# A hybrid attention block with SwiGLU: the down product on scaled f16 halves instead of fp32r

## The chip, the cores and the metric

One core of one Trainium2 chip runs the whole kernel in one launch. The metric is device time in microseconds (us) of that core. Five engines work side by side: TensorE (PE, with PEld for its weight loads), VectorE (DVE), ScalarE (ACT), GpSimd (POOL) and SyncE (SP), which here issues the transfers.

## What is computed

The reference is one encoder block over 2048 tokens (and 16 meta tokens) of width 1024, all in float32. The change concerns the last part, the feed-forward network (FFN) of inner width 2816:

```
h = rms_norm(x, attn_norm_g[l])
proj = jnp.einsum('bld,de->ble', h, w_in[l])
...
mixed = jnp.concatenate([out_a, out_b], axis=-1)
x = x + jnp.einsum('ble,ed->bld', mixed, w_out[l])
h = rms_norm(x, ffn_norm_g[l])
g = jnp.einsum('bld,df->blf', h, w_gate[l])
u = jnp.einsum('bld,df->blf', h, w_up[l])
x = x + jnp.einsum('blf,fd->bld', jax.nn.silu(g) * u, w_down[l])
```

out_a is grouped-query attention of 8 heads, out_b differential attention of 4 heads; both normalise queries and keys and turn them by rotary tables.

## The kernel before

The kernel runs through four stages. Every product of float32 numbers is made of three matmuls on halves: an operand x is cast to a short type (the high half) and the cast's error x − high is cast again (the low half); high·high, high·low and low·high are summed. `split` (L114 to L116) does this: the cast on ACT (L112), the subtract on POOL or DVE (L116). Products on f16 halves need the operands scaled into f16's range, products on fp32r halves don't.

- Input projection (0 to 480 us): 16 token tiles of 128 rows (and one of 16), and for each six units of 384 columns of w_in; `proj` makes 24 matmuls a unit, `post` norms and rotates, and SP stores queries, keys and values to DRAM (L281, L330 to L335).
- Attention (480 to 1670 us), whose order of instructions a planner in the program sets. The change doesn't touch it.
- Output projection (1670 to 1884 us): 16 token tiles, 48 fp32r matmuls each (L1285). Meanwhile the weights w_gate and w_up are read once to find a scale: 32 loads of 704 KB (`squares`, L1238) with an ACT square each that sums along a row (L1239); `weights_scale` (L1243 to L1253) adds up the sums with a matmul against ones and takes a power of two near 1/sqrt of the total (POOL's pow at L1248, then a mask). `wsc` holds it.
- FFN (1884 to 3304 us): two halves b of the tokens (1024 each), and in each 22 tiles f of 128 inner columns, so 44 steps. A step loads w_gate, w_up and w_down of its tile (`wload`, L1323 to L1331: SP loads 512 KB into a raw tile, ACT scales gate and up by `wsc`, ACT casts, POOL subtracts), makes 96 matmuls of 128x512 for gate and up in f16 (L1379), forms silu(g)·u with a tanh on ACT (L1381) and two DVE products (L1382, L1383), splits it into fp32r halves, and multiplies the previous step's tile by its w_down: 48 fp32r matmuls (`down`, L1340), three for each of 16 outputs of 128x512, each of which DVE adds to the running sum y (L1342).

A scheduler orders the instructions of each engine from the program as written, outside the attention, so matmuls of `down` are mixed among those of gate and up. Tiles are given out from rings: four tiles for f16 weights of gate and up, four raw tiles, two for w_down's halves and two for the activation's:

```
rings = dict(w=[er[0], we[0], er[1], wk_[0]], d=[we[1], wk_[1]], a=[we[2], wk_[2]], y=[we[3], wk_[3]],
             r=[slots[id(z)] for t in (NT - 2, NT - 1) for z in mxt[t]])
```

A tile can be written again when its last reader is done: a raw tile after POOL's subtract, a w_down tile after the last matmul of its `down`. Sums of `down` go to a ring of three PSUM tiles (`psD`). The names that the profile shows are those of the memory that a tile lies in: e, kt, qa, qb are also the attention's buffers; qa and qb hold raw weights, e and kt the halves; psd is a sum of `down`, pg one of gate or up, th the activation, pj a projected unit, xt a tile of x, cs the rope table.

## Time and profile before

| what | us |
|---|---|
| median of 3 runs (lowest, highest) | 3316.16 (3311.18, 3320.15) |
| the profiled execution, its own time | 3310.24 |
| span of the profile | 3308.4 |
| PE busy | 3145.7 (95% of the span) |
| PEld, DVE busy | 2069.5, 2056.2 |
| ACT, POOL busy | 1639.2, 1639.3 |

The span is the time from the first to the last instruction of the profiled execution; its own time is 2 us longer. Busy shares are means over stages that differ: the page's slices show PE full from the output projection on, and a granted clock of 0.9 or more of full speed in every slice. The rows below are read stage by stage.

### The profile page before, as it was taken

The numbers are of one execution on the slowest core, as the hardware profiler recorded it, in microseconds if no ns is written. First come the engines' busy times: TensorE is split into PE (matmuls) and PEld (weight loads), VectorE is DVE, ScalarE is ACT, GpSimd is POOL, SyncE is SP. The second block draws the span as 40 slices with busy tenths as digits, with TensorE's granted clock in tenths as the row PEclk, the third lists the DMA queues.
The fourth block names the chain that finished last, engine by engine and source line by source line (L and its number), as shares of the span: only waits on it lengthen the run. The fifth ranks groups of instructions, "written<-read, shape, count | busy, mean of one in ns | idle before, by whom it ended". The sixth has DMA issues, their size and how long they took to land.

```text
span 3308.4 us, 57942 instructions
## 1 busy us (share of the span) xinstructions
PE 3145.7 (95%) x23043; PEld 2069.5 (63%) x23043; DVE 2056.2 (62%) x3656; ACT 1639.2 (50%) x1991; POOL 1639.3 (50%) x1597
## 2 busy tenths in 40 slices
PE   8999988989988898888889999999999999999999
PEld 7999975655555565555568755555555555555555
DVE  7555568888888889888865334444444544444445
ACT  6333328888887888888866222222222322222220
POOL 6888866767676677676721133232232323232231
PEclk9999999999999999999999999999999999999999
DMA  5322233343243334433467511111111511111111
GB/s 168 72 68 68 67 85 74 78 109 88 73 111 81 84 86 100 88 83 74 107 236 259 165 58 55 42 58 42 54 52 45 174 50 51 45 58 39 57 45 51
DMA packets 503359, 281.35 MB, mean 85 GB/s; under 512 B 330704, under 2 KB 478624, under 8 KB 502576
## 3 DMA queue, kind: packets, MB, share of 16 engines
q1 hardware_dynamic: 501376, 275.14, 30.6%
q8 instruction: 181, 2.97, 0.4%
q10 hardware_dynamic: 1712, 2.51, 0.3%
q14 instruction: 90, 0.74, 0.1%
HBM read 168.44 MB, written 39.93 MB: 63 GB/s over the span
## 4 chain that ended last, share of the span: by engine, by line
PE 72%; DVE 11%; ACT 6%; issue 5%; DMA 4%; POOL 1%; SPq 0%; DVEq 0%; ACTq 0%; POOLq 0%
PE pg L1379 27%; PE psd L1340 14%; PE pl L269 10%; PE sy L482 4%; PE ob L594 4%; PE oa L570 3%; DVE e L489 3%; ACT et L555 2%; DVE mna L502 2%; PE ps L1285 2%; PE sy L498 2%; PE sy L512 2%; PE sy L513 2%; DVE e L536 2%; DMA wq<-in_w_up_dram 1%
## 5 line engine op out<-in xcount | busy, mean ns | idle before, releaser
L1342 DVE TENSOR_TENSOR y<-psd,y 128x512 f32<-128x512 f32 x704 | 484.8, 691 | 551.0 <-PE psd L1340 549.8
L561 POOL TENSOR_TENSOR hl<-et,hl 128x1024 f16<-128x1024 f32 (+1 forms) x247 | 520.9, 2128 | 303.8 <-ACT hl L112 168.7
L1379 PE MATMUL pg<-h2h,e 128*128 128x512 f16 x2112 | 660.0, 380 | 1.6 <-POOL e L116 1.6
L1379 PEld LDWEIGHTS <-e 128*128 128x128 f16 x3168 | 283.2, 98 | 390.3 <-issue 84.9
L1379 PE MATMUL pg<-h2l,e 128*128 128x512 f16 x1056 | 400.7, 380 | 0.0
L489 DVE CUSTOM_DVE_ANT_0 e<-sy,zero,mn 128x1024 f32<-128x1024 f32 x256 | 325.5, 1277 | 43.0 <-PE sy L482 37.8
L116 POOL TENSOR_TENSOR e<-qa,e 128x1024 f16<-128x1024 f32 (+1 forms) x44 | 100.0, 2273 | 498.8 <-issue 381.8
L555 ACT ACTIVATE et<-sy,lnpa,ndq 128x1024 f32<-128x1024 f32 (+1 forms) x288 | 322.1, 1145 | 39.6 <-PE sy L513 16.9
L549 POOL TENSOR_TENSOR p<-e,p 128x516 f16<-128x516 f32 (+2 forms) x320 | 311.4, 1006 | 50.7 <-ACT p L112 49.6
L1381 ACT ACTIVATE th<-pg,unh 128x512 f32<-128x512 f32 x88 | 60.5, 688 | 532.3 <-PE pg L1379 525.4
L1340 PE MATMUL psd<-kt,kt 128*128 128x512 f32 x1056 | 323.0, 434 | 0.0
L502 DVE TENSOR_REDUCE mna<-sy 128x1 f32<-128x1024 f32 x256 | 311.3, 1217 | 16.1 <-PE sy L498 15.5
L1340 PE MATMUL psd<-e,e 128*128 128x512 f32 x1056 | 320.5, 432 | 0.7 <-DVE y L1342 0.7
L517 ACT ACTIVATE e<-e,bs,ndq 128x2064 f32<-128x2064 f32 x128 | 269.2, 2103 | 92.2 <-DVE bs L522 92.2
L482 PE MATMUL sy<-kt,qb 128*128 128x512 f16 (+1 forms) x1280 | 284.3, 342 | 30.5 <-DVE mn L489 9.9
L570 PEld LDWEIGHTS <-hl 128*128 128x128 f16 (+1 forms) x6528 | 241.6, 97 | 91.3 <-issue 20.5
L570 PE MATMUL oa<-va,hl 128*128 128x65 f16 (+3 forms) x6528 | 261.8, 193 | 21.0 <-DVE hl L561 7.9
L112 ACT CAST hl<-et 128x1024 f16<-128x1024 f32 (+1 forms) x288 | 275.8, 991 | 6.8 <-PE oa L570 5.3
L116 POOL TENSOR_TENSOR kt<-qb,kt 128x1024 fp32r<-128x1024 f32 x22 | 52.7, 2397 | 442.8 <-issue 384.2
L594 PEld LDWEIGHTS <-pt 128*128 128x128 f16 (+2 forms) x3200 | 202.2, 98 | 72.9 <-issue 7.8
L1340 PEld LDWEIGHTS psd<-e,e 128*128 128x128 f32 x1056 | 198.8, 189 | 59.0 <-DVE y L1342 1.2
L1340 PEld LDWEIGHTS psd<-kt,kt 128*128 128x128 f32 x1056 | 199.0, 189 | 58.5
(229 smaller groups left out, 5775.4 us busy)
## 6 DMA issues: line engine op xcount, KB each, us to landing
wq<-in_w_gate_dram SPq DMA_DIRECT2D x16, 704.0 KB, 4.9
wq<-in_w_up_dram SPq DMA_DIRECT2D x16, 704.0 KB, 5.4
qa<-in_w_gate_dram SPq DMA_DIRECT2D x22, 512.0 KB, 3.9
qa<-in_w_down_dram SPq DMA_DIRECT2D x22, 512.0 KB, 3.7
qa<-in_w_up_dram SPq DMA_DIRECT2D x22, 512.0 KB, 3.8
qb<-in_w_up_dram SPq DMA_DIRECT2D x22, 512.0 KB, 3.7
qb<-in_w_down_dram SPq DMA_DIRECT2D x22, 512.0 KB, 3.6
qb<-in_w_gate_dram SPq DMA_DIRECT2D x22, 512.0 KB, 3.8
```

What stands on the lines that cost most here:

```text
L269: T.matmul(ps[:rows, c0:UW], hb[:, a, k, :rows], w_at(w, ui, k)[:, c0:], start=(k == 0 and a == 0 and w == 0), stop=(k == KD - 1 and a == 1))
L482: T.matmul(y[:, (c - c0) // 512 if g_ else j, :n], qt[:, j, a, qi * P:(qi + 1) * P], kt[:, c:c + n], start=(a == 0), stop=(a == 1))
L489: V.tensor_tensor_reduce(e[:, c0:c1], src[:, :c1 - c0], zero.broadcast_to([P, c1 - c0]), 1.0, mn[:, g_ - 1:g_] if g_ else big, ALU.add, AL ...
L502: V.tensor_reduce(g["mn"][:, h, g_:g_ + 1], y.rearrange("p b n -> p (b n)"), axis=AX.X, op=ALU.min)
L549: eng.tensor_tensor(out=p[:, at + c0:at + c1], in0=st["e"][0][:, c0:c1], in1=p[:, c0:c1], op=ALU.subtract)
L555: A.activation(of(et, k), of(y, k), AF.Exp, bias=lnpa if k else lnpa[:NM], scale=ndq[:, 0:1] if k else ndq[:NM, 0:1])
L561: eng.tensor_tensor(out=of(z[:, 1], k), in0=of(et, k), in1=of(z[:, 0], k), op=ALU.subtract)
L570: T.matmul(o[:, h, :wn], z[:rows, a, i, h * P:(h + 1) * P], vt[:rows, c, vh, :wn], start=(first and h == 0 and n == 0), stop=(last and n = ...
L594: T.matmul(o, pt[:rows, blk, :], vt[:rows, c, vh, :], start=(c == 0 and n == 0), stop=(c == NC - 1 and n == 1))
L1340: T.matmul(ps, a[:, i * P:(i + 1) * P], w[:, 0, ns], start=(ii == 0), stop=(ii == 2))
L1342: V.tensor_tensor(out=yt[:, ns], in0=ps, in1=yt[:, ns], op=ALU.add)
L1379: T.matmul(ps, a[:, k], b_[:, k], start=(k == 0 and ii == 0), stop=(k == KD - 1 and ii == 2))
```

## The change

The squares for the scales move to the input projection. From its 13th pair of unit and token tile on, `squares(3)` runs ahead of each unit: three pieces of 128 KB, one each of w_gate, w_up and w_down, are loaded by SP (L260) into one of two buffers and squared by ACT with a sum per row (L261), 88 of each in all. `weights_scale` runs at the beginning of the output projection and makes two scales: `wsc` for gate and up, `wdsc` for w_down.

`down` works on f16 halves. w_down is scaled by `wdsc` (L1339, one more ACT instruction of 128x1024 a step). The activation tile gets a power of two from its own sum of squares: ACT squares both halves of th (L1396), DVE adds the two sums (L1410), a matmul of 128x1 against ones adds over the partitions into a tile of psD (L1412), DVE bounds it (L1414), POOL takes its pow (L1415), DVE masks, scales, inverts and multiplies (L1416 to L1419), and ACT scales both halves (L1422) before they are split. The eviction (now L1352) multiplies by the inverse scale as it adds. The weights' and activation's halves take f16 tiles of the same rings; th has four buffers, not two; the attention's pool sm2 has 7, not 10.

```diff
+        wqp = ph.enter_context(tc.tile_pool(name="wqp", bufs=2, reuse_waits="tile"))
+        sqs = [(i, n) for n in range(NSQ) for i in range(3)]
+
+        def squares(n):
+
+            for _ in range(min(n, len(sqs))):
+                i, z = sqs.pop(0)
+                w = (w_gate, w_up, w_down)[i].rearrange("(t p) n -> t (p n)", t=NSQ // 11)
+                w = w[z // 11].rearrange("(c n) -> c n", c=11)[z % 11].rearrange("(p n) -> p n", p=P)
+                raw = wqp.tile([P, D * DFF // NSQ // P], F32, name="wq")
+                SP.dma_start(raw, w)
+                A.activation(raw, raw, AF.Square, accum_out=wsq[:, i, z:z + 1])
...
+            if i >= SQ0:
+                squares(3)
             hb, tab, rs = ready[t]
             pj = proj(ui, t, hb, rs)
...
-        sm = ph.enter_context(tc.tile_pool(name="sm2", bufs=10, reuse_waits="tile"))
+        sm = ph.enter_context(tc.tile_pool(name="sm2", bufs=7, reuse_waits="tile"))
...
-            def squares(t):
-
-                rs_, cs_ = slice(t // 2 * P, (t // 2 + 1) * P), slice(t % 2 * (DFF // 2), (t % 2 + 1) * (DFF // 2))
-                for i, w in enumerate((w_gate, w_up)):
-                    raw = wqp.tile([P, DFF // 2], F32, name="wq")
-                    SP.dma_start(raw, w[rs_, cs_])
-                    A.activation(raw, raw, AF.Square, accum_out=wsq[:, t, i:i + 1])
-
             def weights_scale():
 
-                tot = np3.tile([P, 1], F32, name="tot")
-                V.tensor_reduce(tot, wsq.rearrange("p t i -> p (t i)"), axis=AX.X, op=ALU.add)
-                ps = psS.tile([P, 1], F32, name="pss")
+                tot = np3.tile([P, 2], F32, name="tot")
+                V.tensor_reduce(tot[:, 0:1], wsq[:, 0:2], axis=AX.XY, op=ALU.add)
+                V.tensor_reduce(tot[:, 1:2], wsq[:, 2], axis=AX.X, op=ALU.add)
+                ps = psS.tile([P, 2], F32, name="pss")
                 T.matmul(ps, allones, tot, start=True, stop=True)
                 V.tensor_scalar(tot, ps, 1e-30, None, op0=ALU.max)
-                G.tensor_tensor(out=wsc[:, 0:1], in0=tot, in1=mhalf[:, :1], op=ALU.pow)
-                V.tensor_scalar(wsc[:, 0:1].bitcast(I32), wsc[:, 0:1].bitcast(I32), 0x7F800000, None, op0=ALU.bitwise_and)
-                V.tensor_scalar(wsc[:, 0:1], wsc[:, 0:1], 2.0 ** 15, None, op0=ALU.mult)
-                V.reciprocal(wsc[:, 1:2], wsc[:, 0:1])
+                for i, z in enumerate((wsc, wdsc)):
+                    G.tensor_tensor(out=z[:, 0:1], in0=tot[:, i:i + 1], in1=mhalf[:, :1], op=ALU.pow)
+                    V.tensor_scalar(z[:, 0:1].bitcast(I32), z[:, 0:1].bitcast(I32), 0x7F800000, None, op0=ALU.bitwise_and)
+                    V.tensor_scalar(z[:, 0:1], z[:, 0:1], 2.0 ** 15, None, op0=ALU.mult)
+                    V.reciprocal(z[:, 1:2], z[:, 0:1])
...
-                for z in (2 * t, 2 * t + 1) if t < 2 else (t + 2,):
-                    if z < NT:
-                        squares(z)
-                if t == NT - 2:
+                if t == 0:
                     weights_scale()
...
-            tp4 = p4.enter_context(tc.tile_pool(name="tp4", bufs=2, reuse_waits="tile"))
+            tp4 = p4.enter_context(tc.tile_pool(name="tp4", bufs=4, reuse_waits="tile"))
+            sq4 = p4.enter_context(tc.tile_pool(name="sq4p", bufs=1, reuse_waits="tile")).tile([P, 512], BF16, name="sq4")
...
                 dn = name == "d"
-                w = place("d" if dn else "w", [P, 2, 1, D] if dn else [P, 2, KD, P], F32R if dn else F16)
+                w = place("d" if dn else "w", [P, 2, 1, D] if dn else [P, 2, KD, P], F16)
                 raw = place("r", [P, 1, D] if dn else [P, KD, P], F32)
                 SP.dma_start(raw[:, 0] if dn else raw, src)
-                if not dn:
-                    A.activation(raw, raw, AF.Copy, scale=wsc[:, 0:1])
+                A.activation(raw, raw, AF.Copy, scale=(wdsc if dn else wsc)[:, 0:1])
                 split(w[:, 0], w[:, 1], raw, A, G)
                 return w[:, 0], w[:, 1]
...
-                ah, al = act
+                ah, al, un = act
...
-                        V.tensor_tensor(out=yt[:, ns], in0=ps, in1=yt[:, ns], op=ALU.add)
+                        V.scalar_tensor_tensor(yt[:, ns], ps, un, yt[:, ns], op0=ALU.mult, op1=ALU.add)
...
-                    ac_ = place("a", [P, 2, TB * P], F32R)
+                    ac_ = place("a", [P, 2, TB * P], F16)
                     ah, al = ac_[:, 0], ac_[:, 1]
+                    asq = tp4.tile([P, 2], F32, name="asq")
+                    ths = []
...
-                        split(ah[:, ns], al[:, ns], th, A, G)
+                        A.activation(sq4, th, AF.Square, accum_out=asq[:, n:n + 1])
+                        ths.append(th)
...
+                    def scaled():
+
+                        a16 = tp4.tile([P, 1], BF16, name="a16")
+                        V.tensor_tensor(out=a16, in0=asq[:, 0:1], in1=asq[:, 1:2], op=ALU.add)
+                        ps = psD.tile([P, 1], F32, name="psd")
+                        T.matmul(ps, ones16, a16, start=True, stop=True)
+                        sc = tp4.tile([P, 3], F32, name="asc")
+                        V.tensor_scalar(sc[:, 0:1], ps, 1e-30, None, op0=ALU.max)
+                        G.tensor_tensor(out=sc[:, 1:2], in0=sc[:, 0:1], in1=mhalf[:, :1], op=ALU.pow)
+                        V.tensor_scalar(sc[:, 1:2].bitcast(I32), sc[:, 1:2].bitcast(I32), 0x7F800000, None, op0=ALU.bitwise_and)
+                        V.tensor_scalar(sc[:, 1:2], sc[:, 1:2], 2.0 ** 15, None, op0=ALU.mult)
+                        V.reciprocal(sc[:, 2:3], sc[:, 1:2])
+                        V.tensor_scalar(sc[:, 2:3], sc[:, 2:3], wdsc[:, 1:2], None, op0=ALU.mult)
+                        for n in range(2):
+                            ns = slice(n * 512, (n + 1) * 512)
+                            A.activation(ths[n], ths[n], AF.Copy, scale=sc[:, 1:2])
+                            split(ah[:, ns], al[:, ns], ths[n], A, G)
+                        return sc[:, 2:3]
+
                     if prev is not None:
                         down(*prev)
```

Where the order of instructions changes, in three places.

PE, where a step's first gate matmul stands; e and kt are weights' halves, h2h and h2l the tokens'. Before, among six downs and the step's other matmuls:

```order
L1379 MATMUL pg<-h2h_23237,kt_33563 128x512
L1340 MATMUL psd<-e_33359,e_33364 128x512 x6
L1379 LDWEIGHTS e_33767
L1379 MATMUL pg<-h2h_23236,e_33767 128x512
L1379 LDWEIGHTS e_33767
```

With the change:

```order
L1350 LDWEIGHTS e_34299
L1350 MATMUL psd<-e_34293,e_34299 128x512
L1391 LDWEIGHTS e_34962
L1391 MATMUL pg<-h2h_24033,e_34962 128x512
L1391 LDWEIGHTS e_34962
L1391 MATMUL pg<-h2l_24035,e_34962 128x512
L1391 LDWEIGHTS kt_34968
L1391 MATMUL pg<-h2h_24033,kt_34968 128x512
```

The new gate weights (e_34962) are now first used behind 24 gate and up matmuls and 15 downs in a row, which follow the last down of the step before and the matmul against ones; 17 matmuls with the up weights (kt_34968) come right behind the first two.

ACT in the FFN (L1329, L1339 scale weights, L112, L114 cast, L1381, L1393 tanh). Before:

```order
L112 CAST e_32104<-th_32211 128x512
L1329 ACTIVATE qa_32508<-qa_32508,wsc 128x1024
L112 CAST e_32507<-qa_32508 128x1024
L1381 ACTIVATE th_32365<-pg,unh 128x512
L1329 ACTIVATE qa_32724<-qa_32724,wsc 128x1024
L1381 ACTIVATE th_32421<-pg,unh 128x512
L112 CAST kt_32309<-qb_32310 128x1024
L112 CAST kt_32314<-th_32365 128x512
```

With the change:

```order
L1339 ACTIVATE qb_34067<-qb_34067,wdsc 128x1024
L114 CAST e_33385<-qa_33386 128x1024
L1422 ACTIVATE th_33216<-th_33216,asc 128x512
L1422 ACTIVATE th_33271<-th_33271,asc 128x512
L114 CAST kt_33164<-th_33216 128x512
L114 CAST kt_33164<-th_33271 128x512
L1393 ACTIVATE th_33670<-pg,unh 128x512
L1339 ACTIVATE qa_33828<-qa_33828,wsc 128x1024
L1393 ACTIVATE th_33725<-pg,unh 128x512
L114 CAST e_33827<-qa_33828 128x1024
L1396 ACTIVATE sq_25526,asq<-th_33670 128x512
```

The cast of w_down (e_33385) now stands ahead of the activation's scaling and casts, and the scaling and the cast of the gate weights (e_33827) behind them, with a tanh between the two. On POOL, the pow of the new scale (L1415) stands right ahead of w_down's subtract.

SP in the input projection (L260 is the new load; L346 to L351, before L330 to L335, store queries and keys, L297 and L281 values). Before:

```order
L281 DMA v_scr_b_84<-pj 128x128
L184 DMA xt<-in_x_dram 128x1024
L330 DMA q_scr_a_73<-th 128x256 x2
L335 DMA k_scr_a_74<-th 64x2x128
L281 DMA v_scr_b_87<-pj 128x128
L332 DMA q_scr_b_76<-th 128x128 x2
```

With the change:

```order
L260 DMA wq<-in_w_gate_dram 128x256
L346 DMA q_scr_a_73<-th 128x256
L260 DMA wq<-in_w_up_dram 128x256
L346 DMA q_scr_a_73<-th 128x256
L351 DMA k_scr_a_74<-th 64x2x128
L260 DMA wq<-in_w_down_dram 128x256
L260 DMA wq<-in_w_gate_dram 128x256
L297 DMA v_scr_b_87<-pj 128x128
L348 DMA q_scr_b_76<-th 128x128
```

The loads stand between the stores of each unit, three to a unit.

## Rows read from the trace of the kernel before

**Rows 1.** Windows: us, then busy (x instructions) per engine, PEclk, DMA share, GB/s.
```profile
110.00:440.00 330.00, 330.00 (x1991) 327.34 (x1990) 183.40 (x567) 114.03 (x285) 270.42 (x573) 1.00 0.27 66
...
1670.00:1884.00 214.00, 206.37 (x1006) 166.64 (x1007) 105.67 (x177) 106.45 (x166) 28.50 (x29) 0.98 0.67 232
1950.00:2500.00 550.00, 550.00 (x2474) 301.78 (x2472) 237.17 (x344) 134.24 (x154) 154.45 (x85) 1.00 0.16 49
```

**Rows 2.** Waits of PE in the FFN: us in total, times, longest.
```profile
PE pg L1379 <- POOL e L116: 1.6, 1, 1.6
```

**Rows 3.** Timeline of ACT in the FFN, two tanh ten steps apart.
```profile
2193.77 0.69 ACT L1381 ACTIVATE th<-pg,unh 128x512 f32<-128x512 f32 x1 [2.27 <-PE pg L1379]
...
2514.13 0.69 ACT L1381 ACTIVATE th<-pg,unh 128x512 f32<-128x512 f32 x1 [2.23 <-PE pg L1379]
```

**Rows 4.** Timeline of PE, two stretches of the FFN: start us, duration us, instruction.
```profile
2510.03 0.38 PE L1379 MATMUL pg<-h2l,e 128*128 128x512 f16 x1
...
2511.64 0.60 PE L1379 MATMUL pg<-h2h,e 128*128 128x512 f16 x2
...
2525.66 0.59 PE L1379 MATMUL pg<-h2h,e 128*128 128x512 f16 x2
...
2527.39 0.38 PE L1379 MATMUL pg<-h2l,e 128*128 128x512 f16 x1
```

**Rows 5.** Line L1379: its weight loads idle before them (us, times) until:
```profile
  ACT e L112: 5.6, 20
  ACT kt L112: 4.9, 18
```

**Rows 6.** Lines of the FFN by form: count | busy us, mean ns | idle before.
```profile
L1342 DVE TENSOR_TENSOR y<-psd,y 128x512 f32<-128x512 f32 x704 | 484.8, 691 | 551.0 <-PE psd L1340 549.8
...
L116 POOL TENSOR_TENSOR e<-qb,e 128x1024 f16<-128x1024 f32 x44 | 95.0, 2159 | 44.8 <-ACT e L112 44.8
L1383 DVE SCALAR_TENSOR_TENSOR th<-th,unh,pg 128x512 f32<-128x512 f32 x88 | 65.8, 747 | 126.9 <-PE pg L1379 126.6
...
L1329 ACT ACTIVATE qb<-qb,wsc 128x1024 f32<-128x1024 f32 x44 | 50.6, 1150 | 135.2 <-DMA qb<-in_w_gate_dram 68.3 <-DMA qb<-in_w_up_dram 66.9
...
L112 ACT CAST e<-qb 128x1024 f16<-128x1024 f32 x44 | 46.0, 1046 | 20.6 <-PE pg L1379 20.0
L112 ACT CAST e<-th 128x512 fp32r<-128x512 f32 x44 | 27.0, 614 | 6.5 <-DVE th L1383 6.5
```

**Rows 7.** Timeline of SP and ACT: one load of w_gate and its scaling.
```profile
2505.85 0.37 SPq L1327 DMA_DIRECT2D qb<-in_w_gate_dram  x1
...
2509.68 1.15 ACT L1329 ACTIVATE qb<-qb,wsc 128x1024 f32<-128x1024 f32 x1 [3.42 <-DMA qb<-in_w_gate_dram]
```

**Rows 8.** Timeline of the weights' scale in the output projection.
```profile
1814.19 0.15 DVE L1247 TENSOR_SCALAR tot<-pss 128x1 f32<-128x1 f32 x1
...
1814.42 0.56 POOL L1248 TENSOR_TENSOR wsc<-tot,mhalf 128x1 f32<-128x1 f32 x1 [7.28 <-DVE tot L1247]
```

**Rows 9.** DMA issues: transfer, count, KB each, median us to landing.
```profile
xt<-in_x_dram SPq DMA_DIRECT2D x16, 512.0 KB, 3.8
...
qb<-in_x_dram SPq DMA_DIRECT2D x16, 512.0 KB, 5.7
...
cs<-in_rope_dram SPq DMA_DIRECT2D x16, 128.0 KB, 2.3
```

**Rows 10.** Lines of ACT in the input projection, 110 to 440 us.
```profile
L291 ACT ACTIVATE m<-pj 128x256 f32<-128x256 f32 x47 | 20.4, 433 | 0.0
```

**Rows 11.** Tile wq: its instructions, min/median/max ns, first and last start us.
```profile
L1239 ACT ACTIVATION_READ_ACCUMULATOR wq<-wq x32: 180/185/196, 1695.7 to 1800.9; 128x1 f32 x32
```

**Rows 12.** Timeline of SP in the input projection.
```profile
246.75 0.38 SPq L184 DMA_DIRECT2D xt<-in_x_dram  x1
...
252.74 0.86 SPq L332 DMA_DIRECT2D q_scr_b<-th  x2
...
274.29 0.38 SPq L184 DMA_DIRECT2D xt<-in_x_dram  x1
```

More of the change, by code (lines that the diff above doesn't have):

```diff
@@ L49 @@
 SHU = 2.0 ** -12
+NSQ = 88
+SQ0 = 12
 VA, VB, VG = 7, 4, 0
@@ L143, in block_kernel @@
     lnpa = const.tile([P, 1], F32, name="lnpa")
+    wsq = const.tile([P, 3, NSQ], F32, name="wsq")
     dq = const.tile([P, 2], F32, name="dq")
@@ L1188, in block_kernel @@
         V.memset(allones, 1.0)
-        wsq = yp.tile([P, NT, 2], F32, name="wsq")
+        wdsc = yp.tile([P, 2], F32, name="wdsc")
+        ones16 = yp.tile([P, P], BF16, name="ones16")
+        V.memset(ones16, 1.0)
         g2_sb = yp.tile([P, D], F32, name="g2_sb")
@@ L1229, in block_kernel @@
             V.tensor_scalar(g2_sb, g2_sb, gm2[:, 1:2], 2.0 ** 9, op0=ALU.mult, op1=ALU.mult)
-            wqp = p3.enter_context(tc.tile_pool(name="wqp", bufs=2, reuse_waits="tile"))
             psS = p3.enter_context(tc.tile_pool(name="psS", bufs=1, space=PSUM, reuse_waits="tile"))
-            def squares(t):
-                rs_, cs_ = slice(t // 2 * P, (t // 2 + 1) * P), slice(t % 2 * (DFF // 2), (t % 2 + 1) * (DFF // 2))
-                for i, w in enumerate((w_gate, w_up)):
-                    raw = wqp.tile([P, DFF // 2], F32, name="wq")
-                    SP.dma_start(raw, w[rs_, cs_])
-                    A.activation(raw, raw, AF.Square, accum_out=wsq[:, t, i:i + 1])
             def weights_scale():
-                tot = np3.tile([P, 1], F32, name="tot")
-                V.tensor_reduce(tot, wsq.rearrange("p t i -> p (t i)"), axis=AX.X, op=ALU.add)
-                ps = psS.tile([P, 1], F32, name="pss")
+                tot = np3.tile([P, 2], F32, name="tot")
+                V.tensor_reduce(tot[:, 0:1], wsq[:, 0:2], axis=AX.XY, op=ALU.add)
+                V.tensor_reduce(tot[:, 1:2], wsq[:, 2], axis=AX.X, op=ALU.add)
+                ps = psS.tile([P, 2], F32, name="pss")
                 T.matmul(ps, allones, tot, start=True, stop=True)
                 V.tensor_scalar(tot, ps, 1e-30, None, op0=ALU.max)
-                G.tensor_tensor(out=wsc[:, 0:1], in0=tot, in1=mhalf[:, :1], op=ALU.pow)
-                V.tensor_scalar(wsc[:, 0:1].bitcast(I32), wsc[:, 0:1].bitcast(I32), 0x7F800000, None, op0=ALU.bitwise_and)
-                V.tensor_scalar(wsc[:, 0:1], wsc[:, 0:1], 2.0 ** 15, None, op0=ALU.mult)
-                V.reciprocal(wsc[:, 1:2], wsc[:, 0:1])
+                for i, z in enumerate((wsc, wdsc)):
[3 more added lines that the diff above has]
+                    V.reciprocal(z[:, 1:2], z[:, 0:1])
                 V.tensor_scalar(unh[:, 0:1], wsc[:, 1:2], gm2[:, 0:1], 2.0 ** -10, op0=ALU.mult, op1=ALU.mult)
@@ L1393, in block_kernel @@
                                     pre_norm(t)
+                    def scaled():
[15 more added lines that the diff above has]
+                        return sc[:, 2:3]
                     if prev is not None:
                         down(*prev)
-                    prev = (b, f, (ah, al), wd)
+                    prev = (b, f, (ah, al, scaled()), wd)
             down(*prev)
```

## The prediction

> **What bounds the kernel now.** I read the stages first. In the windows of four stages [rows 1] the reader is to see that TensorE (PE) is busy without a gap in the input projection (330.00 of 330.00 us) and in the FFN (550.00 of 550.00), for 206.37 of 214.00 us in the output projection, and less in the attention, which the change leaves alone: there both kernels have the same instructions in the same order on every engine, but for two exchanged transfers. So what counts is what PE executes, and whether it begins to wait.
>
> Next, the FFN. PE's gate and up matmuls wait there 1.6 us in all [rows 2], so its period is PE work. The same tanh stands at 2193.77 and at 2514.13, ten steps apart [rows 3]: 32.04 us a step, 44 steps. A step has 96 gate and up matmuls in f16 and 48 down matmuls in fp32r (the trace writes f32). Eight f16 matmuls begin between 2525.66 and 2527.39 [rows 4]: 1.73 / 8 = 0.216 us each. Between the f16 matmuls that begin at 2510.03 and 2511.64 stand six downs: (1.61 − 0.216) / 6 = 0.232 us each. An fp32r matmul of this size is thus dearer by 0.016 us only.
>
> Third, how much slack the weights have. The loading of gate weights into PE waited 38 times, 10.5 us in all, for the ACT cast of its weights [rows 5], without a loss on PE: the weights come just in time already. That is the place to look at.
>
> **The change, part by part.** The sum is made against the profiled execution, 3310.2 us, which is 6 us under the median of 3316.2.
>
> 1. *PE work of the FFN.* All 144 matmuls of a step in f16: 144 × 0.216 = 31.15 us (0.2163 unrounded) instead of 32.04, so −0.89 × 44 = −39 us. The new matmul of 128x1 (L1412) has no row of its kind; between nothing and one f16 matmul of 512 columns (0.216), I take 0.05: +2 us.
>
> 2. *The chain that loads a step's gate weights.* In the changed order 26 of the 44 steps look alike: the last down of step k−1, the new 128x1 matmul, 24 gate/up and 15 down matmuls, and then the first matmul with newly made gate weights. PE has 40 × 0.216 = 8.7 us of work between the two. In that time this must happen, each link waiting for the one before by its buffers: the last down ends (0.4, its own length [rows 4] and its issue) and frees the f16 tile of w_down; ACT casts the next w_down into it (1.05 [rows 6]); POOL subtracts (2.16 [rows 6]), which frees the raw tile; SP loads the next w_gate into it, and ACT begins to scale it 9.68 − 5.85 = 3.83 us after the issue [rows 7]; ACT scales (1.15), works off a tanh that stands ahead in its order (0.69), and casts (1.05) [rows 6]. The subtract stands behind the pow of the new scale in POOL's order: the down's eviction (0.69, [rows 6]), a maximum (0.15) and the pow (0.56, [rows 8]) end at 0.4 + 0.1 + 0.69 + 0.15 + 0.56 = 1.9 us, 0.4 later than the cast. Together 0.4 + 1.05 + 0.4 + 2.16 + 3.83 + 1.15 + 0.69 + 1.05 = 10.7, with semaphores (some 0.03 a link, an estimate from the gaps in [rows 7]) 10.9 us. PE waits 10.9 − 8.7 = 2.2 us in each: +57 us. Behind the waiting matmul stands all of PE's work, the downs of the last step too, so the wait is not made up. The ends: nothing, if a load is quick (a gain is excluded, since the matmuls are counted in 1); 26 × 3 = 78 us, if each link costs 0.1 more.
>
> 3. *The other 18 steps and the middle*, where the order runs unevenly (9 to 48 downs in a row). The first down of a step needs the chain eviction, maximum, pow, two small DVE steps (0.15 each), the ACT scale of the activation tile and its cast: 0.69 + 0.15 + 0.56 + 0.3 + 0.69 + 0.61 is 3.0, and with the last down's 0.4, the DVE work that stands between (0.69) and hand-overs some 4.2 us after the last down before [rows 6, 8]. Where fewer than 20 other matmuls lie between, PE waits. I take 1.4 us a step: +25; ends 0 and 18 × 2.2 = 40.
>
> 4. *The end of the program.* Before, 96 downs followed one another. Now it is 48 downs, the 128x1 matmul, 48 downs, and again, so two chains of 4.2 us lie bare (8.4), and in three runs of 48 the evictions set the pace: 16 × 0.69 = 11.1 us [rows 6] against 48 × 0.216 = 10.4: 2. Clock and filling for the rest: +16, ends 13 and 21.
>
> 5. *The activation's extra work* (two ACT squares, two ACT scales, five small DVE steps a step of the FFN) and the scaling of w_down (ACT, 1.15): 5 us more of ACT a step. ACT is busy for 134 of 550 us there [rows 1], so it costs nothing but through the chains above. The eviction now takes three operands, as the product at L1383 does (0.75 against 0.69, [rows 6]); three downs last 0.65, but gate matmuls between them leave it room, and the runs of 48 are counted in 4.
>
> 6. *Output projection.* 32 loads and squares go; PE was idle for 214.0 − 206.4 = 7.6 us: −5, ends 0 and −7.6. The weights' scale, now at its start and for two values, has some 190 us before its first use.
>
> 7. *Input projection.* 264 pieces of 128 KB, three to a unit and tile, 88 units. Two buffers: each load waits for the square two before it, and on SP, behind a load that waits, stand the transfers of x, of queries, keys and values. No row shows such a load; the nearest is the rope table's, 128 KB, 2.3 us to landing [rows 9]. A square of 128x256 takes 0.43 [rows 10] and its accumulator's reading 0.185 [rows 11], in part side by side: 0.52. Load, square and hand-over take 2.3 + 0.08 + 0.52 + 0.03 = 2.93 us, and with the transfers and casts that share SP and ACT (0.86 for a pair of query stores alone, [rows 12]) I take 3.3; two buffers make 1.65 us a piece, 4.95 a unit. A tile of six units takes 274.29 − 246.75 = 27.54 us now [rows 12], 4.59 a unit. So +0.36 × 88 = +32 us. Ends: 0, if the round takes at most 3.05; +112, if a load takes 2.9 us to land.
>
> Sum: −39 + 2 + 57 + 25 + 16 − 5 + 32 = +88, 3398; I say **3400 us**, 2.5% above the median. A measurement of this kernel can tell some 0.3% (10 us) from no change.
>
> **The rivals.**
>
> *The projection hides its squares* (a round of 3.05 us or less): 3400 − 32 = 3368. For it speaks that ACT is busy there for only 114 of 330 us [rows 1]; against it, that SP works in order.
>
> *Transfers slow each other.* The same 512 KB of x land in 3.8 us in the projection and in 5.7 in the output projection [rows 9], where the DMA share is 0.67 and not 0.27 [rows 1]. The squares about double the projection's traffic. If a load of 128 KB then lands in 2.6 instead of 2.3, the round is 3.6 and the term +71: 3440; with 2.9, 3480. The Trainium skill says of this (DMA: Bandwidth & Descriptors, "Latency and other measured facts") that memory latency is 0.2 us on average, 2 us at high load, and is most of a transfer's fixed cost. By that rule the extra traffic itself makes each small load later, and an estimate from its two figures (1.8 us more) would put the term past its upper end; the two rows of x agree in direction.
>
> *The chains are covered: faster.* Place: the first gate matmul of a step. If the gate weights land within 3.83 − 2.2 = 1.6 us, or the raw tile comes free 2.2 us earlier, PE never waits in the steady steps; with the squares hidden and point 3 at nothing, the time is 3310 − 39 + 2 − 5 + 10 = 3278. Against it: no load of 512 KB in the kernel lands so soon.
>
> *Half of it.* The chain costs 1 us a step (26), the tail 13, the rest is hidden: 3310 − 37 − 5 + 26 + 13 = 3307, no change.
>
> *The change doesn't do what it says:* f16 downs take 0.232 all the same, since both come from the wait for weights: 3400 + 48 × 44 × 0.016 = 3434. Against it stands the gate's f16 matmul of the same shape.
>
> **How the numbers follow.** Forecast 0.50; squares hidden 0.19; transfers slowed 0.12; covered 0.06; half 0.06; f16 downs as slow 0.07. The first three and the last are slower by over 0.3%: 0.88. Faster 0.06, same 0.06. The range takes the low end of point 3 with hidden squares (3368 − 25 = 3343, so 3345) and, above, a landing of 2.9 us (3475); outside it lie the covered and half cases and some of the slowed.
>
> **What the new profile would show.** Tanh to tanh 33.3 to 33.6 us in the FFN, with weight loads of gate matmuls that wait some 2 us for an ACT cast; six units of the projection in about 29.7 us instead of 27.5, and pieces that land in 2.3 us; an output projection 5 us shorter; f16 downs 0.216 apart; at the end two gaps of 4 us. A period at or under 31.5 would make the chain wrong; projection tiles still at 27.5 the squares.

## The result: slower by 3.4%, and the profile after

The changed kernel takes 3428.8 us (median of 4 runs, 3422.5 to 3430.8) against 3313.7 of the kernel before in the same comparison: ratio 1.034, 95% interval 1.032 to 1.036. The forecast was 3400 and 1.025, slower, by two stages that begin to wait. The profiled execution took 3430.1 us, its span is 3428.3.

Where the time lies is read from the first and last matmuls of each stage. The last one of the input projection stands at 533.3 us instead of 474.6 (+58.7); from there to the first gate matmul of the FFN it is 1404.0 instead of 1409.9 (−5.9, all of it in the output projection, which shrank from 211.4 to 205.2); and from there to the end 1491.0 instead of 1423.9 (+67.1). Together +119.9, the difference of the spans.

The windows of the stages, which answer to [rows 1], in the same columns:

```profile
110.00:440.00 330.00, 295.53 (x1723) 279.53 (x1722) 154.66 (x486) 184.74 (x642) 225.32 (x487) 1.00 0.52 138
1732.00:1937.00 205.00, 203.86 (x1003) 166.67 (x1004) 105.55 (x181) 64.63 (x104) 25.03 (x27) 0.99 0.41 129
1950.00:2500.00 550.00, 525.88 (x2418) 234.55 (x2417) 241.08 (x412) 193.94 (x272) 153.20 (x101) 0.99 0.17 50
```

PE, full before in the first and the last, now lacks 34.5 us of 330 in the projection and 24.1 of 550 in the FFN, at a granted clock of 1.00 and 0.99. So it waits and is hardly slower; where it is slower stands in the last section. In the output projection it waits for almost nothing.

Two tanh ten steps apart (the timeline of ACT, [rows 3]):

```profile
2201.57 0.69 ACT L1393 ACTIVATE th<-pg,unh 128x512 f32<-128x512 f32 x1 [0.81 <-POOL e L118]
...
2531.51 0.69 ACT L1393 ACTIVATE th<-pg,unh 128x512 f32<-128x512 f32 x1 [0.81 <-POOL e L118]
```

329.94 / 10 = 33.0 us a step, where all matmuls together are 144 × 0.2163 = 31.15. The waits of PE in these steps (2220 to 2630 us, twelve steps; total, times, longest):

```profile
PE psd L1350 <- DVE y L1352: 9.9, 12, 0.8
PE pg L1391 <- ACT e L114: 8.4, 12, 0.9
```

Each step waits once for the cast of its gate weights and once for an eviction: 18.3 / 12 = 1.53 us. These rows count from the modelled end of the matmul before, 0.38 us after its start, while the next one would start after 0.216. So each wait costs 0.17 us more than its row says: 1.53 + 2 × 0.17 = 1.86 a step, which is what lies between 31.15 and 33.0. One step's chain, from the timeline of SP, ACT, POOL and PE:

```profile
2493.26 0.17 PE L1412 MATMUL psd<-a,ones 128*128 128x1 bf16 x1
...
2493.46 1.04 ACT L114 CAST e<-qa 128x1024 f16<-128x1024 f32 x1 [7.08 <-PE psd L1412]
...
2494.36 0.55 POOL L1415 TENSOR_TENSOR asc<-asc,mhalf 128x1 f32<-128x1 f32 x1 [12.96 <-DVE asc L1414]
2494.87 2.13 POOL L118 TENSOR_TENSOR e<-qa,e 128x1024 f16<-128x1024 f32 x1
...
2497.03 0.37 SPq L1338 DMA_DIRECT2D qa<-in_w_gate_dram  x1
...
2500.89 1.15 ACT L1339 ACTIVATE qa<-qa,wsc 128x1024 f32<-128x1024 f32 x1 [1.71 <-DMA qa<-in_w_gate_dram]
2501.95 0.67 ACT L1393 ACTIVATE th<-pg,unh 128x512 f32<-128x512 f32 x1
2502.52 1.03 ACT L114 CAST e<-qa 128x1024 f16<-128x1024 f32 x1
...
2503.60 0.39 PE L1391 MATMUL pg<-h2h,e 128*128 128x512 f16 x1 [0.74 <-ACT e L114]
```

Link by link it is the chain of point 2: the cast of w_down, the subtract behind the pow, the load, the scaling, the tanh, the cast, the first gate matmul. The load's issue to ACT's start is 3.86 us (3.83 forecast), the whole 10.3 us from the matmul against ones. (The cast's row names that matmul as its releaser; it begins right behind the last down, whose tile the cast needs.)

In the projection, the pieces (tile wq; landing is the last line, in us):

```profile
L261 ACT ACTIVATE wq<-wq x264: 398/418/440, 14.5 to 482.4; 128x256 f32<-128x256 f32 x132
...
who waited for it (us, times):
  ACT wq L261: 157.5, 151
...
DMA to landing us min/median/max: 1.9/2.2/5.0
```

ACT, in order, waited 157.5 us for pieces, and its own work for the unit stands behind them: from 100 to 535 us DVE waited 120.6 us for ACT's copy of a unit's result. PE's only wait in the window 110 to 440 us is for the values that come out of this, by way of DVE and POOL, and that it transposes at the end of a unit. It is as long as the time that PE lacks there:

```profile
PE pk L336 <- DVE m L323: 34.5, 47, 1.8
```

The loads of x follow each other at 31 to 33 us, not 27.5.

### The profile page after: what moved, and what is told of

Same layout as the page of the kernel before. It is cut to its first block, busy times and chain, and to the rows that moved or that the text cites. A ratio compares the mean times of both kernels' runs of the same rounds, so it can differ in the third digit from the quotient of the medians.

```text
span 3428.3 us, 59471 instructions
## 1 busy us (share of the span) xinstructions
PE 3148.2 (92%) x23087; PEld 1910.0 (56%) x23087; DVE 2110.3 (62%) x3925; ACT 1867.2 (54%) x2763; POOL 1635.8 (48%) x1642
## 4 chain that ended last, share of the span: by engine, by line
PE 40%; ACT 7%; DVE 6%; DMA 6%; issue 4%; POOL 3%; SPq 0%; POOLq 0%; DVEq 0%; ACTq 0%
PE pg L1391 19%; PE psd L1350 9%; PE ps L1295 5%; DMA qb<-in_w_gate_dram 2%; DMA qa<-in_w_gate_dram 2%; PE sy L500 2%; PE oa L588 1%; ACT e L114 1%; PE ob L612 1%; POOL kt L118 1%; POOL e L118 1%; ACT et L573 1%; DVE e L554 1%; DVE e L507 1%; DVE mna L520 1%
## 5 line engine op out<-in xcount | busy, mean ns | idle before, releaser
L1352 DVE SCALAR_TENSOR_TENSOR y<-psd,asc,y 128x512 f32<-128x512 f32 x704 | 500.0, 746 | 515.5 <-PE psd L1350 480.4
L1391 PE MATMUL pg<-h2h,e 128*128 128x512 f16 x2112 | 645.4, 379 | 25.1 <-ACT e L114 24.2
L1391 PEld LDWEIGHTS <-e 128*128 128x128 f16 x3168 | 305.3, 98 | 406.5 <-ACT e L114 40.8
L1350 PE MATMUL psd<-e,e 128*128 128x512 f16 x1056 | 267.9, 387 | 31.1 <-ACT e L114 15.7
L114 ACT CAST hl<-et 128x1024 f16<-128x1024 f32 (+1 forms) x288 | 275.8, 991 | 6.8 <-PE oa L588 5.3
L1350 PE MATMUL psd<-kt,kt 128*128 128x512 f16 x1056 | 262.5, 382 | 18.4 <-DVE y L1352 14.5
L1415 POOL TENSOR_TENSOR asc<-asc,mhalf 128x1 f32<-128x1 f32 x44 | 24.2, 551 | 524.2 <-DVE asc L1414 524.2
L612 PE MATMUL ob<-vb,pt 128*128 128x128 f16 (+2 forms) x3200 | 233.2, 220 | 1.8 <-DMA pt<-p 1.7
L530 PE MATMUL sy<-qa,kt 128*128 128x512 f16 (+1 forms) x544 | 207.7, 382 | 22.9 <-DVE mn L507 10.0
L1391 PE MATMUL pg<-h2h,kt 128*128 128x512 f16 x704 | 220.5, 383 | 0.0
L285 PE MATMUL pl<-e,hb 128*128 128x384 f32 (+1 forms) x782 | 218.5, 340 | 1.3 <-ACT e L210 0.6
```

The lines of the kernel that those rows point to most:

```text
L114: (A.copy if eng is A else eng.tensor_copy)(o, i)
L612: T.matmul(o, pt[:rows, blk, :], vt[:rows, c, vh, :], start=(c == 0 and n == 0), stop=(c == NC - 1 and n == 1))
L1350: T.matmul(ps, a[:, i * P:(i + 1) * P], w[:, 0, ns], start=(ii == 0), stop=(ii == 2))
L1352: V.scalar_tensor_tensor(yt[:, ns], ps, un, yt[:, ns], op0=ALU.mult, op1=ALU.add)
L1391: T.matmul(ps, a[:, k], b_[:, k], start=(k == 0 and ii == 0), stop=(k == KD - 1 and ii == 2))
```

## The experiments

All times are medians against the kernel before of the same comparison; a stage's length is read as above.

**1. The two halves apart.** First the move of the squares alone, with the FFN of the kernel before:

```diff
-                w = place("d" if dn else "w", [P, 2, 1, D] if dn else [P, 2, KD, P], F16)
+                w = place("d" if dn else "w", [P, 2, 1, D] if dn else [P, 2, KD, P], F32R if dn else F16)
...
-                    prev = (b, f, (ah, al, scaled()), wd)
+                    prev = (b, f, (ah, al), wd)
```

> The squares' move alone: the input projection and output projection of the change, with the FFN of the kernel before (down in fp32r, no activation scale; the scale for w_down is made and not used). Theory (the two halves of the change cost by themselves and add up): the projection ends 59 us later, the output projection is 6 us shorter, the FFN's steps are 32.0 us again: about 3366 us, ratio 1.016. Rival (the squares' move also costs the FFN something, or the FFN's loss needs it): the FFN is not back at 1424 us and the time is above 3375.

Measured 3374.0 us, ratio 1.018 (1.017 to 1.020). FFN 1426.7 us, at 32.1 a step (32.0 before); projection 537.6, 4 us later than in the change; these 4 and the FFN's 3 are most of what lies between 3366 and 3374. No wait of the FFN came with the move (PE's waits there sum to 1.7 us). Then the FFN alone, as an edit of the kernel before:

```diff
+        V.memset(wdsc[:, 0:1], 2.0 ** 9)
+        V.memset(wdsc[:, 1:2], 2.0 ** -9)
...
+                    prev = (b, f, (ah, al, scaled()), wd)
```

> The FFN of the change alone: input and output projection as before, squares of w_gate and w_up in the output projection; the sum over w_down is left out and its scale is a constant. Theory (the parts add): projection as before (27.5 us a tile), FFN 67 us longer with steps of 33.0 us: about 3381 us, ratio 1.020. Rival (the FFN's loss comes from elsewhere, such as the memory that the squares' buffers took): about 3314 us plus less than 40.

3383.8 us, ratio 1.021 (1.018 to 1.024); FFN 1493.9, projection 472.0. And the change without pieces:

```diff
+    V.memset(wsq[:, 0:2], D * DFF / D / P / NSQ)
+    V.memset(wsq[:, 2], D / P / NSQ)
...
-            if i >= SQ0:
-                squares(3)
```

> The change without any load or square of the weights: the sums of squares are set to constants. Theory: all of the projection's 59 us go, tiles of six units take 27.5 us again, the FFN stays as it is: about 3370 us, ratio 1.017. Rival (part of the projection's lengthening comes from something else in the change): tiles stay above 28.5 us.

3370.9 us, 1.018 (1.016 to 1.020); tiles of 27.5, FFN 1488.9. Two losses, then, each in its stage. By the medians they are 59.3 and 69.1 us alone and 115.1 together; the two sum to 13 more, which by the spans lies in 2 to 4 us in each of their stages and has no place of its own.

**2. Why the pieces cost.** Four buffers instead of two, first in the memory of the attention's query tiles:

```diff
-        wqp = ph.enter_context(tc.tile_pool(name="wqp", bufs=2, reuse_waits="tile"))
+        wring = ['qa0', 'qa1', 'qb0', 'qb1']
...
+                raw = slot(wring[0], [P, D * DFF // NSQ // P], F32)
```

> The change with four buffers for the pieces of the weights instead of two (they lie in the attention's query tiles, which are idle then). Theory (the round of two buffers, load, square and hand-over, sets the projection's pace): a round may take 6 us now, and the tiles come back to 27.5 to 28 us: about 3372 us. First rival (the instructions themselves, 264 loads in SP's order and 264 squares in ACT's, set the pace): tiles stay at 31 to 32 us and the time at about 3425. Second rival (more traffic makes all transfers late): pieces land later than 2.5 us and the time stays above 3410.

A miss, 3540.1 us (1.068): the expectation was mistaken about the memory. Those tiles hold halves of w_in almost until the projection ends, so the pieces waited for that (the first square in qa stands at 438.3): the projection ended at 474.0, as without pieces, and from there to the first gate matmul it took 1575.4 us instead of 1409.9. The window right after the projection, with the same columns as above, shows PE idle for most of it:

```profile
440.00:700.00 260.00, 72.71 (x470) 50.45 (x469) 71.35 (x167) 168.06 (x591) 49.20 (x69) 0.65 0.57 160
```

So the edit was repeated with free memory:

```diff
-        sqx = c1.tile([P, D], BF16, name="sqx")
...
-        wqp = ph.enter_context(tc.tile_pool(name="wqp", bufs=2, reuse_waits="tile"))
+        wqp = ph.enter_context(tc.tile_pool(name="wqp", bufs=4, reuse_waits="tile"))
...
+            A.activation(xt[:rows], xt[:rows], AF.Square, accum_out=ss[:rows])
```

> The change with four buffers for the pieces of the weights instead of two, this time in memory that is truly free: the square of x that is thrown away goes into x's own tile, and its old tile's memory to the buffers. Theory (the round of two buffers, load, square and hand-over, sets the projection's pace): tiles of six units come down from 32 to 28 us or less and the time to 3370 to 3385. Rival (the 264 loads and squares themselves, in SP's and ACT's fixed orders, set the pace): tiles stay at 31 us or more and the time above 3415.

3398.2 us, 1.027 (1.025 to 1.028): between the two. Tiles took 34.2 and 31.3, then 28 to 30 us while pieces ran, and 26 to 27 when they were through, at 350 us. The window 110 to 340 us of tile wq alone counts them (us, ACT's busy time and instructions, PEclk, DMA share, GB/s; a piece is two ACT instructions); the first row is the changed kernel, the second this run:

```profile
110.00:340.00 230.00, 68.93 (x274) 1.00 0.51 137
```

```profile
110.00:340.00 230.00, 92.08 (x390) 0.99 0.66 175
```

137 pieces against 195: 1.68 us each, or 3.36 for a round of two buffers, against 1.18. The buffers do set the pace of the pieces. But the freed pieces crowd: nothing ties a piece to its unit, and 4.2 of them ran in each unit's time, ahead of ACT's own work. So a tie was added (a column of ones made from the unit's result is the square's scale):

```diff
-                A.activation(raw, raw, AF.Square, accum_out=wsq[:, i, z:z + 1])
+                A.activation(raw, raw, AF.Square, scale=one, accum_out=wsq[:, i, z:z + 1])
...
+                one = sm.tile([P, 1], F32, name="one")
+                V.tensor_scalar(one, pj[:, 0:1], 0.0, 1.0, op0=ALU.mult, op1=ALU.add)
+                squares(3, one)
```

> The change with four buffers as in the run before, and the squares held to three a unit: each square's scale operand is a column of ones made from the unit's own result, so no square can run ahead of its unit. Theory (two buffers and the crowding of squares ahead of their units make the projection long; three pieces a unit fit beside 4.59 us of PE work): tiles of six units at 27.5 to 28.2 us, projection as without squares, time 3368 to 3382. Rival (three loads and squares a unit don't fit beside the unit's own stores and casts, with any buffers): tiles at 29 us or more, time above 3392.

3378.4 us, 1.020 (1.018 to 1.022); tiles at 27.5 after the first few, projection 475.7. Three pieces a unit are hidden entirely. The same tie with the two buffers of the change:

> The change with its two buffers, and the squares held to three a unit by the column of ones as in the run with four buffers. It tells the two edits of that run apart. Theory (the round of two buffers sets the pace): a round of 3.5 us for two pieces gives 5.3 us for three, so tiles of six units stay at 31 to 33 us and the time at 3415 to 3445. Rival (squares that crowd ahead of their units were the cause, and pacing is the cure): tiles at 27.5 to 28.5 us and 3370 to 3385 us.

3427.1 us, 1.034 (1.033 to 1.036); tiles of 29.4 to 32.8, projection 521.7, 133 pieces in the window (1.73 us each). PE in the window 110 to 380 us, four buffers and then two:

```profile
110.00:380.00 270.00, 270.00 (x1628) 267.92 (x1627) 149.17 (x525) 181.89 (x592) 222.20 (x468) 1.00 0.58 154
```

```profile
110.00:380.00 270.00, 246.54 (x1446) 237.78 (x1446) 136.14 (x469) 169.42 (x529) 195.52 (x415) 0.99 0.53 138
```

The one with the greater DMA share is the one that doesn't wait. So it is neither the traffic nor the count of instructions. Against the 474.6 us of the kernel before, the projection is longer by 59 to 71 us with two buffers unpaced (the five runs that have them, the change among them; this stage's order of instructions is the same in all five), by 47 with two paced, by 25 with four unpaced, and by 1 with four paced. Both edits are needed, and the buffers carry most.

**3. Why the FFN's weights come late.** One line moved, so that a step's scale is written ahead of the last step's product:

```diff
+                    un = scaled()
                     if prev is not None:
                         down(*prev)
-                    prev = (b, f, (ah, al, scaled()), wd)
+                    prev = (b, f, (ah, al, un), wd)
```

> One line of the change moved: a step's activation scale is written ahead of the previous step's down product instead of behind it. All work and all buffers stay. Theory (the order as the change writes it makes the downs run one step later than before, so that the two w_down tiles and the four raw tiles have no slack, and that costs the FFN): downs lag as before, the waits for the gate weights go, steps take 31.2 to 31.6 us instead of 33.0, the FFN about 1395 to 1410 instead of 1491, the time 3335 to 3350. Rival (the work of the scale itself, on ACT, DVE and POOL, makes the steps long): steps stay above 32.5 us and the time above 3400.

3356.8 us, 1.013 (1.012 to 1.015). The FFN took 1403.5 us, 87.5 less, in the expected band; the time is above its band by the projection, which ended at 545.8 this time. The waits of PE from 2220 to 2630 us again, all of them (thirteen steps now):

```profile
PE psd L1350 <- DVE y L1352: 1.0, 2, 0.5
```

The waits for the gate weights are gone, with every instruction of the scale still there. The order of PE shows what moved. Counted in it, for the steady steps: how many steps of gate and up matmuls have been issued, from a step's own on, when its down product begins; and how many matmuls PE has between the down that frees a w_down tile and the first matmul of the gate weights that wait for it:

| kernel | steps of gate and up matmuls ahead of the product | matmuls from the freeing down to the waiting gate matmul |
|---|---|---|
| before | 2.0 | 162 |
| the change | 3.0 | 40 |
| this run | 2.3, growing to 2.8 | 114, falling to 54 |
| constant scale (below) | 2.0 | 162 |
| four w_down tiles (below) | 3.0 | over 160 |

In the change a step's matmul against ones takes its PSUM tile behind the previous product's, and each product runs a whole step later than before. There are w_down tiles for two steps and raw tiles for four loads, three of which are a step's. With the later product, the cast of w_down has to wait for the last down just run, and the raw tile that it frees is the very one that the next gate weights need. (By the rings, the last down of step j frees the tile of w_down j+2, and that one's raw tile goes to the gate weights of step j+4.) The chain takes 10.56 us from the start of that last down, which is 49 matmuls of 0.2163: it doesn't fit into 40 and, if it is as long there, fits into 54. The expectation had the downs lag as before; they don't, and less slack than before is still enough.

A constant in place of the scale:

```diff
-                        T.matmul(ps, ones16, a16, start=True, stop=True)
...
-                        A.activation(sq4, th, AF.Square, accum_out=asq[:, n:n + 1])
...
+                        sc = csc
```

> The change with a constant for the activation's scale: the two squares, their sum, the matmul against ones, the maximum, the pow and the four small steps are left out; the two ACT scalings stay. Theory (the chain of waits comes from the position that the scale gives to the downs): the order falls back to the even mix of the kernel before, steps take 31.2 to 31.6 us, the end has no gaps, the time is 3325 to 3345. Rival (w_down's new scaling on ACT and the f16 tiles alone make the weights late): steps stay at 32.5 us or more, time above 3395.

3336.6 us, 1.007 (1.005 to 1.009), as expected. The order of PE falls back to that of the kernel before; steps of 31.1 us, FFN 1385.5. So f16 downs do give what the rows promised, 38 us (1423.9 − 1385.5), if they are not made to wait, and the scale with its order, as in the run before, costs 1403.5 − 1385.5 = 18, none of it in the steady steps. Then room for four w_down tiles, in the order of the change:

```diff
+                        z = place("d", [P, 2, 2, 1, D], F16)
+                        dpair.extend([z[:, 0], z[:, 1]])
```

> The change with room for four steps' w_down halves instead of two (two steps share a tile of the old size, as f16 needs half of fp32r's bytes). Theory (in the chain of point 2 the cast of w_down waits for the last down of the step before): with another tile free the cast, the subtract and the load behind them run earlier, the waits for gate weights in the steady steps fall from 1.6 us to under 0.5, steps take 31.3 to 32 us, the time is 3365 to 3395. Rival (another link holds the load, such as the subtract that stands behind the pow, or the raw tiles): steps stay within 0.3 us of 33.0 and the time above 3415.

3405.8 us, 1.029 (1.027 to 1.030), above the expected band and below the rival's. Half: the FFN is 32 us shorter (1459.3), steps take 31.5 and 33.0 by turns. PE's waits in the steady stretch have no row for gate weights any more, so the tile of w_down is a link of the chain; other waits took part of its place (the evictions, and w_down's own halves):

```profile
PE psd L1358 <- DVE y L1360: 4.9, 12, 0.4
PE psd L1358 <- POOL e L118: 2.2, 6, 0.4
PE psd L1358 <- ACT kt L114: 1.9, 6, 0.3
```

**4. Versions that beat both.** The moved line with the squares split between the stages (w_gate and w_up in the output projection as before, one tied piece of w_down a unit in the input projection):

```diff
+            if i >= SQ0:
+                squares_d(1, one)
...
+                    un = scaled()
```

> A version meant to beat both: the scale written ahead of the previous down product (as in the run of that name), the squares of w_gate and w_up in the output projection as in the kernel before, those of w_down in the input projection, one piece a unit, two buffers, paced by the unit's result. Theory (the terms add): projection 475, attention and output projection 1410, FFN 1404: 3288 to 3295 us, ratio 0.993 to 0.995. Rival (one piece a unit still lengthens the projection by 10 us or more): 3300 us or more, no gain.

3296.9 us, ratio 0.995 (0.993 to 0.996), 2 us above the band. And the moved line with all squares tied and four buffers, the edits of the two runs above together:

> A second version meant to beat both: all squares in the input projection with four buffers and paced, and the scale written ahead of the previous down product. Theory (if the paced squares are hidden): projection 475, attention and output projection 1404, FFN 1404: 3282 to 3292 us, ratio 0.991 to 0.994. Rival (the projection stays long): 3305 us or more.

3292.0 us, 0.994 (0.992 to 0.995). Both are faster than the kernel before by more than the 0.3%, by terms that add: in the second, projection 477.3, FFN 1404.6. The time from the projection's end to the FFN is 1417.2 there and 1415.6 in the first, 7 and 6 more than before. It lies in the attention, 1211.6 and 1203.8 us against 1198.5, which these edits don't touch; the profiled execution of the second is the slowest of its six (3301.0). Why is left open.

## Why the prediction was right, point by point

Direction, both places and both mechanisms were as forecast, and the range held; the size was 115 us instead of 84 against the medians. By the spans it is 119.9 against the sum's 88. Of these 32 the projection makes 27 and point 3 makes 10, and the chain gives 5 back. By the terms:

1. *PE work*: right. The run with the constant scale has steps of 31.1 us against 31.15 forecast. The new 128x1 matmul costs less than the 0.05 us taken: it begins at 2493.26 and the next gate matmul at 2493.29.

2. *The chain*: right in every link, a little long. From the start of the last down (2493.04, one matmul of 0.22 ahead of the one against ones) to the gate matmul it took 10.56 us, forecast 10.9. A step lost 33.0 − 31.15 = 1.85 us instead of 2.2, and 28 steps ran evenly: 52 instead of 57. About half of a step's wait shows not at the gate matmul but six downs earlier, at the tenth of the 15 downs. There the evictions stand on DVE behind the two products of silu(g)·u, until the three PSUM tiles of `psD` are full:

```profile
2499.21 0.69 DVE L1394 SCALAR_TENSOR_TENSOR th<-th,pg 128x512 f32<-128x512 f32 x1 [3.48 <-ACT th L1393]
2499.93 0.75 DVE L1395 SCALAR_TENSOR_TENSOR th<-th,unh,pg 128x512 f32<-128x512 f32 x1
2500.60 2.06 DVE L1352 SCALAR_TENSOR_TENSOR y<-psd,asc,y 128x512 f32<-128x512 f32 x3
...
2501.40 1.47 PE L1350 MATMUL psd<-kt,kt 128*128 128x512 f16 x6 [0.83 <-DVE y L1352]
```

By the rows this wait adds nothing to the chain: the cast of the gate weights ends at 2503.55 either way. With four w_down tiles it is the largest that is left.

3. *The uneven steps and the middle*: the term that was mis-sized in the FFN. Forecast 25. Against the run with the constant scale the FFN lost 1491.0 − 1385.5 = 105.5 us; less 52 for the even steps and 18 for the end, some 35 are left, about 15 of them in the first steps and 20 in the middle. The mechanism was the forecast one, waits of downs for their halves and of gate matmuls for theirs, in steps where the slack of 40 matmuls falls to 22. What the term left out is the clock: behind four of these waits it fell, which cost some 9 us (last section). The lengths of single steps say little here: two of the four intervals between tanh of 37 us or more lose next to nothing and are long because more matmuls run in them (174 and 172 instead of 144).

4. *The end*: forecast 16; measured 6.1 + 3.9 of gaps and 5.8 in two runs of 48 downs that took 13.36 and 13.26 us, not 10.4, with 1.8 of waits in the first of the three: 18.

```profile
3393.34 13.36 PE L1350 MATMUL psd<-e,e 128*128 128x512 f16 x48 [6.13 <-ACT e L114]
3406.53 0.17 PE L1412 MATMUL psd<-a,ones 128*128 128x1 bf16 x1
3410.61 13.26 PE L1350 MATMUL psd<-kt,kt 128*128 128x512 f16 x48 [3.90 <-ACT kt L114]
```

5. and 6. *Extra ACT work, output projection*: right for ACT (no wait of its own) and for the output projection (−5.9 against −5). Of the evictions point 5 weighed only their length, 0.75 against 0.65, not what stands ahead of them on DVE (point 2 above).

7. *The projection*: right mechanism, term too small, +32 against +58.7; this is most of the miss. The step that failed is "4.95 a unit. ... So +0.36 × 88". The price of a piece was nearly right (1.65 forecast, 137 pieces in 230 us: 1.68), and so was the landing (2.3, measured 2.2). But it took three pieces for each unit. In the order that ran, pieces go ahead of their units: from the 37th piece, at 103.0 us, to the last, at 482.4, 227 pieces pass while PE gets from its 20th unit to its 92nd, 3.16 a unit. So a unit took 5.28 us and lost 0.69, not 0.36. The delay against the kernel before grows from 3.4 us at unit 20 to 51.6 at unit 90; the other 7 come in one stretch where the pieces end, with a single wait of 5.5 us. The last eight units lose nothing.

Of the rivals, the one that hides the projection's squares fell (it needs the third and fourth buffer and the tie), and so did slowed transfers: at a DMA share of 0.52 the pieces landed in 2.2 us, and only with four buffers, at 0.66, in 2.6. Loads of x did land later, 4.3 instead of 3.8 us. The Trainium skill's rule that memory latency is 0.2 us on average and 2 us at high load (DMA: Bandwidth & Descriptors, "Latency and other measured facts") agrees in direction for those loads and not for the change's pieces; in the projection no median grew by anything near the 1.8 us between its two figures. "Covered" and "half" fell with the chain's rows, and "f16 downs as slow" with the run with the constant scale.

## What to carry to other kernels

Where a loop's tiles come from short rings, an added step can cost more by where it is written than by its work: here it made each product a step late, and moving one line gave 87 us back with nothing left out. Count the work between the instruction that frees a tile and the one that waits for it, and hold it against the length of the chain between them. Before a stream of small loads is put beside full work, compare the round of its buffers (landing, use, hand-over) with the work it is to hide behind, and tie it to that work, or an engine that works through a fixed order will run it ahead and stand. Memory that looks idle by its name may be in use: look at what its tile holds in that stage.

## What was not expected of the hardware

After the end's gap of 6.13 us PE's granted clock stood at 0.50, then rose. Windows of the runs of downs (granted clock is the third number from the end):

```profile
3393.30:3397.00 3.70, 3.66 (x9) 1.34 (x10) 0.46 (x1) 0.50 (x1) 2.27 (x2) 0.50 0.00 0
3397.00:3402.00 5.00, 5.00 (x19) 1.92 (x18) 4.75 (x8) 0.00 (x0) 0.00 (x0) 0.81 0.00 0
3402.00:3406.70 4.70, 4.70 (x23) 2.04 (x21) 4.70 (x8) 0.00 (x0) 0.00 (x0) 1.00 0.01 3
```

0.50 is the lower of the two levels, 1.2 of 2.4 GHz: nine matmuls in the first 3.7 us, twenty-three in the last 4.7. In the fastest version above PE stood 0.38 us before its 48 downs, the window behind shows 1.00 throughout, and the run took 10.71 us instead of 13.36:

```profile
3273.29 10.71 PE L1351 MATMUL psd<-e,e 128*128 128x512 f16 x48 [0.38 <-DVE y L1353]
```

So each of the two gaps of 4 and 6 us at the end cost itself and some 2.6 us more. The prediction had this only as "clock and filling for the rest", without a row; that its 5.6 us come near these 5.2 is luck.

The same happened at four places in the FFN of the changed kernel, each at or shortly behind PE waits of over 2 us in the uneven steps: for 3.4 us from 1968.8 and from 2200.9, and for 6.8 us from 2661.7 and from 2880.1. Behind the waits of the even steps, 0.9 us at most in the second row's stretch, the clock stayed at 1.00:

```profile
2200.90:2204.30 3.40, 2.89 (x8) 0.88 (x6) 1.97 (x3) 0.99 (x2) 1.75 (x2) 0.50 0.53 154
2225.00:2630.00 405.00, 386.65 (x1790) 172.95 (x1788) 183.31 (x323) 142.25 (x200) 113.93 (x75) 1.00 0.16 47
```

By the starts of their matmuls the four cost some 9 us besides the waits. The run with the constant scale has no such stretch in its FFN until its last 2 us, when the matmuls are done.
